# Products over 64 rows of contraction widened to all 128 rows, in a two-layer attention and mLSTM kernel

## The chip, the cores and the metric

The kernel runs on one core of a Trainium2 chip. The metric is the device time of one execution in microseconds (us); smaller is better. The engines of the core are called PE (TensorE, matrix products), DVE (VectorE), ACT (ScalarE), POOL (GpSimd) and SP (SyncE, which issues the DMAs).

## The reference

Two layers over 512 latent tokens and 256 context tokens of width 1024. Layer 0 mixes tokens by two kinds of attention side by side (8 heads of MLA, and 8 query heads of GQA over 2 key heads of dimension 64), layer 1 by a bidirectional mLSTM of 8 heads with keys of dimension 64 and values of dimension 128. Each layer ends with a gated convolutional FFN. Only the latent tokens are returned. The parts that matter here:

```python
def gqa(q, k, v):                        # per key head: 4 query heads, d = 64
    s = einsum('bqgrd,bsgd->bgrqs', q, k) * 64 ** -0.5
    return einsum('bgrqs,bsgd->bqgrd', softmax(s), v)

# mLSTM, one chunk of one direction; C, n is the state before the chunk
s   = einsum('bhtd,bhsd->bhts', qc, kc) * exp(logw - m_t)
num = w_inter * einsum('bhvd,bhtd->bhtv', C, qc) + einsum('bhts,bhsv->bhtv', s, vc)
den = w_inter * einsum('bhd,bhtd->bht', n, qc) + sum(s)
h   = num / max(abs(den), exp(-m_t))
```

## The kernel before

Every operand of a product is held as two tiles, a high part rounded to the matmul's format and a low part with what is left (`split`, L39). A full product of two such operands takes three passes: high by high, low by high and high by low. Projections (`fm`, L78, and `tm`, L89) do this with 128 rows of contraction in each pass.

Where the contraction is only 64 long (a head's dimension in GQA and the mLSTM), two of the three passes are done at once: the query tile holds the high part in 64 rows and the low part in the other 64 (`QE` and `QO` in GQA; the tiles `q` of each head of a pair in the mLSTM), and the high key tile (`KH`, `k`) holds the same high key in both halves. One product with 128 rows gives (high + low) query by high key. The third pass, high query by low key, is a product with 64 rows: `KL` in GQA, `kl` in the mLSTM, and `Sl`, the low part of the mLSTM's state. For even heads the high query stands in rows 0 to 63, for odd heads in rows 64 to 127, and the low tile's half is chosen to match. In GQA `kprep` (L667) already writes the low key to both halves: DVE makes rows 0 to 63 (L675), POOL copies them to 64 to 127 (L676). In the mLSTM one tile `kl` holds the low keys of two heads, one in each half (L925), and `Sl` (L1195) is filled in the half of its head.

The attention (`attend`, L484) is a software pipeline of units; a unit is 256 queries of one head, and a head has two latent units (keys of all 768 tokens) and one context unit (256 keys). Per block of 128 queries a unit makes the scores in PSUM (L424), the negated row maximum on DVE (L427), the exponentials on ACT (L432), a reciprocal on DVE (L434) and the scaling on POOL (L435). Two units later PE transposes the weights (L447), which ACT and DVE split, and three units later PE multiplies them by the values (L469). Between units PE makes the projections that MLA needs next (L95). All 8 GQA heads come first, then the 8 MLA heads, whose scores have 96 rows of contraction and three passes.

The mLSTM (`odd`, L866) works on one head in chunks of 128 tokens: `m_intra` makes the weights within the chunks (a mask from the tiles `tri` is added in PSUM at L1144; the key products are L1154), `m_state` the states before each chunk, and `m_inter` (L1204) the numerators: six products within the chunk (L1212), one by the high state (L1214) and one by the low (L1215). Projections of the next pair of heads and parts of the output projection lie between them as fills (L85, L95, L1103).

A scheduler behind the tile framework sets the order of the instructions on each engine and the semaphores they wait for. Tiles of a pool take over the space of earlier tiles, and where they do, the first writer waits for the last user of that space.

Of the kernel before, what the change touches and what calls it, by code (L numbers as in the profile page):

```python
# [10 lines left out]
F32R = mybir.dt.float32r  # L11
I32 = mybir.dt.int32
BF16 = mybir.dt.bfloat16
# [3 lines left out]
PSUM = bass.MemoryType.PSUM  # L17
SUB, ADD, MUL, MAX, MIN = ALU.subtract, ALU.add, ALU.mult, ALU.max, ALU.min
# [10 lines left out]
def f32(ap):  # L29
    return ap.bitcast(F32)  # L30


class Kernel:
# [14 lines left out]
    def wtile(self, tag, n, cols, dt):  # L48
        """A weight tile: some buffers are permanent, one more of each kind (pool wx) is there when there is room."""
        bufs = [(self.wp, tag + "0"), (self.wp, tag + "1"), (self.wx, tag + "x")]  # L50
        if tag == "wr":
            del bufs[1]
        if self.wx is None:
            bufs.pop()
        self.turn[tag] = self.turn.get(tag, -1) + 1
        pool, nm = bufs[self.turn[tag] % len(bufs)]
        return pool.tile([128, n, cols], dt, tag=nm, name=tag, bufs=1)
# [54 lines left out]
    def B(self, tags):  # L112
        """A PSUM bank, in turn one of the tags: tiles of one tag are taken in program order."""
        self.turn[tags] = self.turn.get(tags, -1) + 1
        tag = tags[self.turn[tags] % len(tags)]
        return self.pp.tile([128, 512], F32, tag=tag, bufs=1, name="ps" + tag)

# [34 lines left out]
    def first_norm(self, pool, X, hh, hl):  # L152
# [63 lines left out]
        # the query projection for GQA goes along, chunk by chunk: one bank for each token tile  # L216
# [78 lines left out]
    def ffn(self, l, X, hh, hl, pool, nt, extra, swap=None, after=None):  # L295
# [4 lines left out]
        a = {}  # L300
        ytile = lambda: pool.tile([128, D], F32, tag="y", name="y", bufs=3)[:, 0:nt]

        def up(f):
            # before the first down products all banks are free for these
            alone = f < 4 and f % 2 == 1

            def banks(tags):
                if alone:
                    return [self.B(tg)[:, 0:n] for tg, (_, n) in zip(tags, segs)]
                p = self.A()  # L310
                return [p[:, t0:t0 + n] for t0, n in segs]

            def halves(ps):
                if nt == T or f >= 4:
                    return [(p, t0, n) for p, (t0, n) in zip(ps, segs)]
                return [(ps[0][:, t0:t0 + n], t0, n) for t0, n in seg2]

            g, v = banks("TU"), banks("RO")
            self.fm(halves(g), self.weights(i["wup"][l, f, 0], KD, 128), (hh, hl), KD)
            self.fm(halves(v), self.weights(i["wup"][l, f, 1], KD, 128), (hh, hl), KD)  # L320
            y = ytile()
            self.conv(y, g, [cw[:, j, f:f + 1] for j in range(3)], cb[:, f:f + 1], segs)
            nc.scalar.activation(y, y, AF.Silu)
            for p, (t0, n) in zip(v, segs):
                nc.vector.tensor_tensor(y[:, t0:t0 + n], y[:, t0:t0 + n], p, op=MUL)
            ah = pool.tile([128, nt], F32R, tag="ah", name="ah", bufs=8)
            al = pool.tile([128, nt], F32R, tag="al", name="al", bufs=8)
            self.split(ah, al, y)
            a[f] = (ah, al)
# [37 lines left out]
        for gi, fs in enumerate(groups):  # L367
            while done < min(NF, fs[-1] + 2):
                up(done)
                done += 1  # L370
                if extra:
                    # its scratch is a y tile, so that it keeps pace with the ups
                    extra.pop(0)(pool.tile([128, D], F32, tag="y", name="y", bufs=3))
            if gi == len(groups) - 1 and swap:
                swap()
            down(fs, gi == len(groups) - 1)
# [122 lines left out]
    def even_tables(self):  # L499
# [4 lines left out]
        # rope tables with the gains folded in  # L504
# [35 lines left out]
    def even(self, hh, hl, acc):  # L540
# [12 lines left out]
        # GQA, token-major  # L553
# [47 lines left out]
        # latents, feature-major  # L601
# [45 lines left out]
        # rope for the shared key part  # L647
# [12 lines left out]
        # while there is little room, the scores' exponentials take the place of the third weight buffers  # L660
# [19 lines left out]
        # GQA attention  # L680
        units = []
        for pr in range(4):
# [20 lines left out]
            units += self.head_units(lambda hd=hd, kv=kv: [(hd["q"][0], KH[kv]), (hd["q"][0][0:64], KL[kv][0:64])],  # L703
                                     V, OT, 4 + pr, 0, {3: [lambda prep=prep: prep([(0, NL)])],
                                                        2: [lambda prep=prep: prep([(NL, NX)])]})
            units += self.head_units(lambda hd=hd, kv=kv: [(hd["q"][1], KH[kv]), (hd["q"][1][64:128], KL[kv][64:128])],
                                     V, OT, 4 + pr, 64)

        # MLA inputs, in steps of one token tile
# [41 lines left out]
        def kvpair(p, pd):  # L751
            k = VM = ss = wk = None

            def step(t):
                nonlocal k, VM, ss, wk
                if t == 0:
                    wk = self.weights(i["w_kvb"][p], 2, 256, kvag)
                    # the keys also go to the space of the query latents, of which both groups are made by then,
                    # the values there and to that of the GQA values
# [56 lines left out]
        # MLA attention: the space of the first head is that of the GQA queries, of the others that of the GQA heads  # L816
# [49 lines left out]
    def odd(self, hh, hl, OT, RP, HP, xs):  # L866
        nc, i = self.nc, self.i
        H = (hh, hl)
        # gates: rows i_f 0.., f_f 32.., i_b 64.., f_b 96..
# [9 lines left out]
        # exponents are kept where the source comes no later (backward: no earlier) than the target; sources on partitions  # L879
        self.tri = []  # L880
        for sg in (1, -1):
            m = RP.tile([128, NT, 128], BF16, tag=f"tri{sg}", name="tri")
            nc.vector.memset(m, 0.0)
            nc.gpsimd.affine_select(m, m, pattern=[[0, NT], [sg, 128]], base=0, channel_multiplier=-sg,
                                    compare_op=ALU.is_ge, fill=-1.0e30)
            self.tri.append(m.rearrange("p q t -> p (q t)"))
# [9 lines left out]
        nc.sync.dma_start(cbs, i["ml_cb"])  # L896
        def proj(hp, pd):
            def qk(w01):
# [4 lines left out]
                if w01:  # L903
                    pd["kl"] = QP.tile([128, NL], F32R, tag="kl", name="kl", bufs=1)
                pd["qk"[w01]] = tiles
                for t0, m in segs:
# [4 lines left out]
                    # twice silu(y), as y (1 + tanh(y / 2))  # L911
# [3 lines left out]
                    for j, (a, b) in enumerate(((slice(0, 64), slice(64, 128)), (slice(64, 128), slice(0, 64)))):  # L915
# [3 lines left out]
                        if w01 == 0:  # L919
                            nc.scalar.mul(t[a], y[a], 0.5)  # L920
                            nc.vector.scalar_tensor_tensor(t[b], y[a], 0.5, f32(t[a]), op0=MUL, op1=SUB)
                        else:
                            nc.scalar.mul(t[a], y[a], 0.0625)
                            nc.gpsimd.tensor_scalar(t[b], y[a], 0.0625, 1.0, op0=MUL, op1=MUL)
                            nc.vector.scalar_tensor_tensor(pd["kl"][a, t0:t0 + m], y[a], 0.0625, f32(t[a]), op0=MUL, op1=SUB)  # L925
                if w01:
                    # the keys with tokens on partitions
# [6 lines left out]
            def v(t):  # L934
                if t == 0:
                    pd["wv"] = self.weights(i["w_mv"][hp], KD, 256)
                    # with a column of ones, which gives the sums
# [21 lines left out]
        with self.tc.tile_pool(name="gates", bufs=1, reuse_waits="tile") as GP:  # L959
# [54 lines left out]
            # per row and tile: the exponents of the weights in the state (ctx as one chunk) and of its decay  # L1014
# [15 lines left out]
            # in the order of the tokens: rows of the backward direction turn round  # L1030
# [34 lines left out]
        # slots of a quarter of a head: the fills make the projections, the gates and the first part of the output  # L1065
# [7 lines left out]
        # from here on nothing reads the normed input: its space takes X and the gated heads  # L1073
# [59 lines left out]
    # the mLSTM of one head, in chunks of 128 tokens, with ctx as one chunk that only makes the first state  # L1133
    def m_intra(self, h, pool, heads, pds, oh, MX, Y, WI, EM, SW, DEC):
        """Within the chunks: the weighted scores, sources on partitions, for both directions."""
# [14 lines left out]
        passes = ((pd["k"][j], pd["q"][j]), (pd["kl"][a], pd["q"][j][a]))  # L1150
# [11 lines left out]
    def m_state(self, h, pool, heads, pds, oh, MX, Y, WI, EM, SW, DEC):  # L1162
        """The states before each chunk of both directions, with the sums in the last column."""
# [28 lines left out]
        Sh, Sl = [pool.tile([128, 4, 2, 130], F32R, tag=f"S{x}", name="S" + x, bufs=1) for x in "hl"]  # L1192
# [5 lines left out]
    def m_inter(self, h, q, pool, heads, pds, oh, MX, Y, WI, EM, SW, DEC):  # L1198
        """One chunk: the part within it plus the state's, for both directions."""
# [15 lines left out]
        nc.tensor.matmul(o, pd["q"][j][a, c], Sl[a, q].rearrange("p d v -> p (d v)"), start=False, stop=True)  # L1215
# [4 lines left out]
    def m_norm(self, h, pool, heads, pds, oh, MX, Y, WI, EM, SW, DEC):  # L1220
        """The numerators over the denominators, both directions summed."""
# [14 lines left out]
    def m_scale(self, h, pool, heads, *_):  # L1236
        """The norm of each token of a head."""
# [19 lines left out]
    def build(self):  # L1257
        tc, nc, i = self.tc, self.nc, self.i
        with ExitStack() as es:
# [54 lines left out]
            # layer 0 mixer  # L1314
# [20 lines left out]
            # layer 0 FFN  # L1335
# [40 lines left out]
            # layer 1 mixer  # L1376
# [26 lines left out]
            # layer 1 FFN  # L1403
# [108 lines left out]
```

## Time and profile before

| | us |
|---|---|
| median of 3 runs | 1812.19 |
| lowest, highest run | 1805.2, 1812.53 |
| span of the profiled execution | 1806.8 |

The page gives no time of the profiled execution beside its span.

| engine | busy us | share of the span | instructions |
|---|---|---|---|
| PE | 1735.2 | 96% | 9615 |
| DVE | 1247.4 | 69% | 2285 |
| ACT | 737.5 | 41% | 1369 |
| POOL | 325.6 | 18% | 357 |

The mean granted clock of PE is 0.977 of full speed. In order of time: conditioning and the first norm to about 165, GQA to about 322, MLA to about 450, the output projection and the FFN of layer 0 to about 1090, gates and first projections of layer 1 to 1158, the mLSTM to 1400, then the last output products and the FFN of layer 1. In the chain of work that ended last, PE has 74% of the span, DVE 10%, POOL 6% and ACT 5%.

A matmul row shows the start, the duration and, as "64*128 64x512", the rows and columns of the weights and of the streamed operand. Durations of matmuls overlap, since they are pipelined, so two neighbouring starts tell more than a duration. In a table by stretch, busy time is given for each engine, with the number of instructions.

### The profile page before, as it was taken

The numbers are of one execution on the slowest core, as the hardware profiler recorded it, in microseconds if no ns is written. First come the engines' busy times: TensorE is split into PE (matmuls) and PEld (weight loads), VectorE is DVE, ScalarE is ACT, GpSimd is POOL, SyncE is SP. The second block draws the span as 40 slices with busy tenths as digits, with TensorE's granted clock in tenths as the row PEclk, the third lists the DMA queues.
The fourth block names the chain that finished last, engine by engine and source line by source line (L and its number), as shares of the span: only waits on it lengthen the run. The fifth ranks groups of instructions, "written<-read, shape, count | busy, mean of one in ns | idle before, by whom it ended". The sixth has DMA issues, their size and how long they took to land.

```text
span 1806.8 us, 25310 instructions
## 1 busy us (share of the span) xinstructions
PE 1735.2 (96%) x9615; PEld 1461.1 (81%) x9622; DVE 1247.4 (69%) x2285; ACT 737.5 (41%) x1369; POOL 325.6 (18%) x357
## 2 busy tenths in 40 slices
PE   6898989999999999999999998999999999999998
PEld 1687768888878888888888887788887898888886
DVE  6896687998868658575867548777777854544444
ACT  3333677889333222121212225645444442232231
POOL 5733254544140000000000005112010210000000
PEclk9898899999999999999999999899998999999999
DMA  8341000000625335242534222111112222323232
GB/s 282 132 153 44 10 11 3 23 1 28 252 71 175 118 105 162 90 151 87 164 106 129 70 73 80 47 48 47 59 35 84 82 94 94 95 94 103 94 103 84
DMA packets 68317, 166.28 MB, mean 92 GB/s; under 512 B 8290, under 2 KB 30818, under 8 KB 67810
## 3 DMA queue, kind: packets, MB, share of 16 engines
q1 hardware_dynamic: 68194, 164.66, 28.2%
q8 instruction: 76, 1.25, 0.3%
q14 instruction: 45, 0.37, 0.1%
q10 hardware_dynamic: 2, 0.01, 0.0%
HBM read 160.44 MB, written 4.20 MB: 91 GB/s over the span
## 4 chain that ended last, share of the span: by engine, by line
PE 74%; DVE 10%; POOL 6%; ACT 5%; issue 4%; DMA 1%; SPq 0%; POOLq 0%; ACTq 0%; DVEq 0%
PE psS L85 30%; PE psT L343 7%; PE psU L343 7%; PE psU L85 3%; PE S L424 3%; PE psR L85 3%; PE psT L85 2%; PE psO L469 2%; PE psR L95 2%; PE psR L343 2%; PE psO L343 2%; PE psU L95 1%; PE psT L95 1%; POOL hl L281 1%; PE psU L1103 1%
## 5 line engine op out<-in xcount | busy, mean ns | idle before, releaser
L85 PE MATMUL psS<-hl,wh 128*128 128x512 f32 (+1 forms) x992 | 348.4, 352 | 3.5 <-POOL hl L281 3.3
L85 PE MATMUL psS<-hh,wh 128*128 128x512 f32 (+1 forms) x992 | 347.1, 351 | 0.4 <-ACT hh L277 0.4
L85 PE MATMUL psS<-hh,wl 128*128 128x512 f32 (+1 forms) x992 | 347.0, 350 | 0.0
L42 ACT CAST wh<-wr 128x1024 fp32r<-128x1024 f32 (+2 forms) x187 | 193.5, 1036 | 358.6 <-PE psO L343 141.3
L43 DVE TENSOR_TENSOR wl<-wr,wh 128x1024 fp32r<-128x1024 f32 (+2 forms) x187 | 229.5, 1228 | 49.4 <-ACT wh L42 48.8
L85 PEld LDWEIGHTS psS<-hl,wh 128*128 128x128 f32 x992 | 187.3, 189 | 31.5 <-POOL hl L281 5.8
L85 PEld LDWEIGHTS psS<-hh,wh 128*128 128x128 f32 x992 | 187.4, 189 | 26.3 <-ACT hh L277 0.7
L85 PEld LDWEIGHTS psS<-hh,wl 128*128 128x128 f32 x992 | 187.4, 189 | 25.3
L291 DVE SCALAR_TENSOR_TENSOR y<-psS,fcw,y 128x511 f32<-128x511 f32 (+1 forms) x60 | 39.5, 658 | 145.5 <-ACT y L289 145.5
L138 DVE CUSTOM_DVE_ANT_0 y<-ar,cb 128x1024 f32<-128x1024 f32 x112 | 136.5, 1219 | 0.0
L261 POOL TENSOR_TENSOR sa<-sa,sq 128x256 f32<-128x256 f32 (+1 forms) x18 | 18.3, 1017 | 648.2 <-ACT sq L260 648.2
L289 ACT ACTIVATE y<-psS,fcb,fcw 128x512 f32<-128x512 f32 (+1 forms) x60 | 40.3, 705 | 207.2 <-PE psS L85 207.2
L378 DVE SCALAR_TENSOR_TENSOR X<-psU,mod,X 128x512 f32<-128x512 f32 (+1 forms) x69 | 48.0, 696 | 91.8 <-PE psU L343 78.9
L435 POOL TENSOR_SCALAR p<-p,rs 128x768 f32<-128x768 f32 (+1 forms) x96 | 73.9, 775 | 134.1 <-DVE rs L434 92.2
L138 DVE CUSTOM_DVE_ANT_0 junk<-ar,cb 128x1024 f32<-128x1024 f32 x64 | 84.0, 1313 | 0.4
L343 PE MATMUL psT<-ah,wh 128*128 128x512 f32 (+1 forms) x184 | 71.7, 390 | 2.2 <-DVE X L378 1.2
L343 PE MATMUL psU<-ah,wh 128*128 128x512 f32 (+1 forms) x184 | 71.5, 388 | 1.2 <-DVE X L378 1.2
L343 PE MATMUL psU<-ah,wl 128*128 128x512 f32 (+1 forms) x184 | 71.0, 386 | 0.0
L343 PE MATMUL psT<-ah,wl 128*128 128x512 f32 (+1 forms) x184 | 71.0, 386 | 0.0
L343 PE MATMUL psT<-al,wh 128*128 128x512 f32 (+1 forms) x184 | 70.9, 386 | 0.0
L343 PE MATMUL psU<-al,wh 128*128 128x512 f32 (+1 forms) x184 | 70.8, 385 | 0.0
L427 DVE TENSOR_REDUCE nm<-S 128x1 f32<-128x768 f32 x64 | 60.3, 946 | 15.0 <-PE S L424 14.7
(664 smaller groups left out, 4387.7 us busy)
## 6 DMA issues: line engine op xcount, KB each, us to landing
ar<-in_ada SPq DMA_DIRECT2D x88, 512.0 KB, 3.6
wr<-in_wup SPq DMA_DIRECT2D x88, 512.0 KB, 3.5
wr<-in_wdn SPq DMA_DIRECT2D x44, 512.0 KB, 3.4
pr<-in_adak SPq DMA_DIRECT2D x16, 256.0 KB, 6.5
wr<-in_w_out SPq DMA_DIRECT2D x8, 512.0 KB, 3.6
wr<-in_w_mqk SPq DMA_DIRECT2D x8, 512.0 KB, 3.4
wr<-in_w_mv SPq DMA_DIRECT2D x8, 512.0 KB, 3.6
wr<-in_w_mo SPq DMA_DIRECT2D x8, 512.0 KB, 3.5
```

What stands on the lines that cost most here:

```text
L42: nc.scalar.copy(hi, src)
L43: nc.vector.tensor_tensor(lo, src, f32(hi), op=SUB)
L85: nc.tensor.matmul(ps, a, b[:, k, x0:x0 + n], start=i == 0, stop=i == 3 * nk - 1)
L95: nc.tensor.matmul(ps, a[:, k, t * 128:(t + 1) * 128], b, start=i == 0, stop=i == 3 * nk - 1)
L138: nc.vector.tensor_tensor_reduce(out, raw, self.cb[:, c], 1.0, 0.0, MUL, ADD, self.mraw[l][:, n, c:c + 1])
L289: nc.scalar.activation(y[:, t0:t0 + n], p, AF.Identity, bias=b, scale=w[1])
L291: nc.vector.scalar_tensor_tensor(y[:, t0 + 1:t0 + n], p[:, 0:n - 1], w[0], y[:, t0 + 1:t0 + n], op0=MUL, op1=ADD)
L343: nc.tensor.matmul(ps[:, 0:n], x[:, off:off + 128], y[:, t0:t0 + n], start=m == 0, stop=m == 3 * nf - 1)
L378: self.nc.vector.scalar_tensor_tensor(X[:, o, t0:t0 + n], ps[:, 0:n], self.mod[l][:, g0 + o, c:c + 1], X[:, o, t0:t0 + n], op0=MUL, op1=ADD)
L424: nc.tensor.matmul(s[:, c0:c0 + n], q[:, q0:q0 + 128], k[:, k0 + c0:k0 + c0 + n], start=m == 0, stop=m == len(passes) - 1)
L427: nc.vector.tensor_reduce(nm, s[:, 0:nk], axis=AX.X, op=MAX, negate=True)
L435: nc.gpsimd.tensor_scalar(p[:, 0:nk], p[:, 0:nk], r, 1.0, op0=MUL, op1=MUL)
```

## The change

The low products of GQA, the low key products and the low state products of the mLSTM are issued over all 128 rows. In GQA both halves of `KL` hold the same low key, so the product also takes in low query by low key. In the mLSTM two tiles `kl` and two tiles `Sl` (one of each for even and one for odd heads) are made once and live through the layer; the half that a head does not write is set to zero once, by POOL. `Sl` no longer comes from the pool of the heads' tiles, and there are two of them in turn where there was one. The mask `tri` is kept for one chunk of 128 columns and not four, and read four times over as a broadcast operand.

The diff also removes comments and docstrings, which are left out here; line numbers after the change are up to 9 higher.

```diff
@@ even
-            units += self.head_units(lambda hd=hd, kv=kv: [(hd["q"][0], KH[kv]), (hd["q"][0][0:64], KL[kv][0:64])],
+            units += self.head_units(lambda hd=hd, kv=kv: [(hd["q"][0], KH[kv]), (hd["q"][0], KL[kv])],
...
-            units += self.head_units(lambda hd=hd, kv=kv: [(hd["q"][1], KH[kv]), (hd["q"][1][64:128], KL[kv][64:128])],
+            units += self.head_units(lambda hd=hd, kv=kv: [(hd["q"][1], KH[kv]), (hd["q"][1], KL[kv])],
@@ odd
-            m = RP.tile([128, NT, 128], BF16, tag=f"tri{sg}", name="tri")
+            m = RP.tile([128, 128], BF16, tag=f"tri{sg}", name="tri")
             nc.vector.memset(m, 0.0)
-            nc.gpsimd.affine_select(m, m, pattern=[[0, NT], [sg, 128]], base=0, channel_multiplier=-sg,
+            nc.gpsimd.affine_select(m, m, pattern=[[sg, 128]], base=0, channel_multiplier=-sg,
                                     compare_op=ALU.is_ge, fill=-1.0e30)
-            self.tri.append(m.rearrange("p q t -> p (q t)"))
+            self.tri.append(m.unsqueeze(1).to_broadcast([128, NT, 128]))
...
+        half = lambda j: slice(64 - 64 * j, 128 - 64 * j)
+        self.kl = [RP.tile([128, NL], F32R, tag=f"kl{j}", name="kl") for j in range(2)]
+        self.Sl = [RP.tile([128, 4, 2, 130], F32R, tag=f"Sl{j}", name="Sl") for j in range(2)]
+        for j in range(2):
+            nc.gpsimd.memset(f32(self.kl[j][half(j)]), 0.0)
+            nc.gpsimd.memset(f32(self.Sl[j][half(j)]), 0.0)
...
-                    pd["kl"] = QP.tile([128, NL], F32R, tag="kl", name="kl", bufs=1)
+                    pd["kl"] = self.kl
...
-                            nc.vector.scalar_tensor_tensor(pd["kl"][a, t0:t0 + m], y[a], 0.0625, f32(t[a]), op0=MUL, op1=SUB)
+                            nc.vector.scalar_tensor_tensor(self.kl[j][a, t0:t0 + m], y[a], 0.0625, f32(t[a]), op0=MUL, op1=SUB)
@@ m_intra
-        passes = ((pd["k"][j], pd["q"][j]), (pd["kl"][a], pd["q"][j][a]))
+        passes = ((pd["k"][j], pd["q"][j]), (pd["kl"][j], pd["q"][j]))
@@ m_state
-        Sh, Sl = [pool.tile([128, 4, 2, 130], F32R, tag=f"S{x}", name="S" + x, bufs=1) for x in "hl"]
+        Sh, Sl = pool.tile([128, 4, 2, 130], F32R, tag="Sh", name="Sh", bufs=1), self.Sl[j]
@@ m_inter
-        nc.tensor.matmul(o, pd["q"][j][a, c], Sl[a, q].rearrange("p d v -> p (d v)"), start=False, stop=True)
+        nc.tensor.matmul(o, pd["q"][j][:, c], Sl[:, q].rearrange("p d v -> p (d v)"), start=False, stop=True)
```

The order of the instructions on PE is the same, row by row. What differs there is a wait, at the first products of GQA (`S` is the score tile, `QE` the queries of an even head):

```order
 L693 MATMUL psU<-ident,QR 128x128
 L424 MATMUL S<-KH,QE 128x512 [waits DVE_49]
-L424 MATMUL S<-KL,QE 128x512
+L424 MATMUL S<-KL,QE 128x512 [waits Pool_49]
 L424 MATMUL S<-KH,QE 128x256
-L424 MATMUL S<-KL,QE 128x256
+L424 MATMUL S<-KL,QE 128x256 [waits Pool_49]
 L424 MATMUL S<-KH,QE 128x512
 L424 MATMUL S<-KL,QE 128x512
```

Nothing moved; the first two low products now wait for POOL as well.

On POOL, at the norm in front of layer 1 (`sa` is the sum of squares of the norm; `Id`, `Fd`, `rm` and `rn` are tables of the gates that are cleared), the piece of the difference reads:

```order
 L261 TENSOR_TENSOR sa<-sa,sq 128x256 [waits Activation_49]
-L965 MEMSET Id 64x768 [waits PE_49]
-L965 MEMSET Fd 64x768
-L965 MEMSET rm 64x768
+L974 MEMSET Id 64x768 [waits DVE_49,PE_49]
+L974 MEMSET Fd 64x768
+L974 MEMSET rm 64x768
 L261 TENSOR_TENSOR sa<-sa,sq 128x256 [waits Activation_49,Pool_49]
```

The order is the same; the clearing of `Id` lies in other space and waits for DVE and for another product of PE.

Later on POOL, between the end of that norm (`hl`) and the first keys (`qk`) of the mLSTM, before:

```order
L281 TENSOR_TENSOR hl<-v,hh 128x256 [waits Activation_49,Pool_49]
L884 AFFINE_SELECT tri<-tri 128x512 [waits DVE_49] x2
L924 TENSOR_SCALAR qk<-cy 64x512 [waits DVE_49,Pool_49]
L924 TENSOR_SCALAR qk<-cy 64x512
L1168 TENSOR_TENSOR kw<-kt,SW 128x768 [waits DVE_49,Activation_49,Pool_49]
```

and after:

```order
L281 TENSOR_TENSOR hl<-v,hh 128x256 [waits Activation_49,Pool_49]
L903 MEMSET kl 64x512 [waits DMAHW6_49,DMAHW1_49,Pool_49]
L884 AFFINE_SELECT tri<-tri 128x128 [waits DVE_49,Pool_49]
L884 AFFINE_SELECT tri<-tri 128x128 [waits DVE_49]
L904 MEMSET Sl 64x1040 [waits Pool_49]
L903 MEMSET kl 64x512
L904 MEMSET Sl 64x1040 [waits PE_49]
L933 TENSOR_SCALAR qk<-cy 64x512 [waits DVE_49]
```

Four clearings are new in front of the keys, and the masks are a quarter as wide.

## Rows read from the trace of the kernel before

**Rows 1.** Timeline of PE in MLA: start us, us, engine, line, operation, tiles, shapes.

```profile
339.43 0.28 PE L424 MATMUL S<-th,tl 96*128 96x256 f32 x1
339.55 0.28 PE L424 MATMUL S<-tl,th 96*128 96x256 f32 x1
```

**Rows 2.** Timeline of PE in GQA, at full clock.

```profile
210.19 0.38 PE L424 MATMUL psR<-KL,QO 64*128 64x256 f32 x1
210.19 0.38 PE L424 MATMUL S<-KL,QE 64*128 64x256 f32 x1
210.50 0.50 PE L424 MATMUL S<-KH,QE 128*128 128x512 f32 x1
210.93 0.50 PE L424 MATMUL S<-KL,QE 64*128 64x512 f32 x1
211.36 0.38 PE L424 MATMUL S<-KH,QE 128*128 128x256 f32 x1
211.67 0.38 PE L424 MATMUL S<-KL,QE 64*128 64x256 f32 x1
```

**Rows 3.** Stretches: us; PE, PEld, DVE, ACT, POOL busy (instructions); clock, DMA, GB/s.

```profile
171.60:196.00 24.40, 24.40 (x58) 15.47 (x59) 11.20 (x26) 9.63 (x21) 4.54 (x6) 0.52 0.00 0
196.00:212.00 16.00, 15.97 (x95) 12.39 (x93) 10.15 (x20) 12.09 (x27) 5.10 (x6) 1.00 0.01 2
212.00:247.00 35.00, 29.91 (x182) 23.27 (x181) 32.07 (x72) 26.12 (x65) 17.38 (x22) 1.00 0.04 12
247.00:303.00 56.00, 55.45 (x307) 43.33 (x307) 40.92 (x94) 40.89 (x99) 24.57 (x30) 0.97 0.04 9
303.00:322.00 19.00, 17.17 (x108) 13.38 (x109) 18.41 (x45) 13.93 (x36) 11.00 (x13) 1.00 0.05 16
1158.00:1400.00 242.00, 238.46 (x1397) 201.67 (x1405) 177.25 (x366) 117.70 (x262) 38.44 (x37) 0.97 0.17 53
```

**Rows 4.** Timeline of PE in GQA, at the lower clock.

```profile
184.64 0.79 PE L424 MATMUL S<-KL,QE 64*128 64x512 f32 x1
185.36 0.58 PE L424 MATMUL S<-KH,QE 128*128 128x256 f32 x1
```

**Rows 5.** Stretches, KL alone: us; PE, PEld, DVE, POOL; clock, DMA, GB/s.

```profile
171.60:196.00 24.40, 9.39 (x14) 4.00 (x14) 0.00 (x0) 0.00 (x0) 0.52 0.00 0
196.00:212.00 16.00, 3.45 (x9) 1.47 (x9) 1.00 (x2) 0.24 (x1) 1.00 0.01 2
212.00:247.00 35.00, 6.45 (x17) 2.75 (x16) 0.09 (x1) 0.70 (x2) 1.00 0.04 12
247.00:303.00 56.00, 13.54 (x32) 5.83 (x32) 0.00 (x0) 0.00 (x0) 0.97 0.04 9
```

**Rows 6.** Timeline of POOL, with the idle time before and its end in brackets.

```profile
168.84 0.95 POOL L676 CAST KL<-KL 64x512 fp32r<-64x512 f32 x2 [17.05 <-DVE KL L675]
...
1134.60 1.70 POOL L924 TENSOR_SCALAR qk<-cy 64x512 fp32r<-64x512 f32 x2 [17.74 <-DVE cy L914]
```

**Rows 7.** Timeline of PE in the mLSTM.

```profile
1355.52 0.33 PE L1154 MATMUL psT<-qk,kl 64*128 64x128 f32 x1
1355.77 0.33 PE L1154 MATMUL psT<-qk 128*128 128x128 f32 x1
...
1363.62 0.33 PE L1214 MATMUL num<-Sh,qk 128*128 128x260 f32 x1
1363.89 0.38 PE L1215 MATMUL num<-Sl,qk 64*128 64x260 f32 x1
1364.20 0.33 PE L1212 MATMUL num<-V,Dh 128*128 128x130 f32 x1
```

**Rows 8.** Timeline of PE and POOL at the norm in front of layer 1.

```profile
1088.37 0.73 POOL L965 MEMSET Id<- 64x768 f32 x1
...
1089.12 0.28 PE L343 MATMUL psU<-ah,wl 128*128 128x256 f32 x1
...
1091.42 0.73 POOL L261 TENSOR_TENSOR sa<-sa,sq 128x256 f32<-128x256 f32 x1 [0.96 <-ACT sq L260]
```

## The prediction

> **What bounds the kernel now.** The page says TensorE (PE) is busy for 96% of the span, and that share hides the question, because a matmul that waits for the array to drain counts as busy. So I read the timeline of PE first and look at starts, not at durations. Where all neighbours use the same rows, the next matmul starts as soon as the array has taken the columns of the last: 0.12 us apart for 256 columns, with 96 rows of contraction [rows 1]; 512 columns then take 0.24. The low-key products of GQA use 64 rows between products that use 128, and there the starts are 0.43 us apart behind a 512-column product and 0.31 behind a 256-column one, both on the way in (KH to KL) and on the way out (KL to KH) [rows 2]. Each change of the number of rows costs 0.19 us in which no column enters.
>
> Next I read the busy times by stretch, since a gain on PE is worth nothing where another engine sets the pace. In the GQA attention (171.6 to 322) PE is busy nearly throughout, but VectorE (DVE) is at 32.07 of 35 us in 212 to 247 and at 18.41 of 19 in 303 to 322, while it has slack in the other stretches [rows 3]. In the mLSTM (1158 to 1400) PE is busy 238.46 of 242 us against 177.25 for DVE and 117.70 for ScalarE (ACT) [rows 3]: the end of that stretch is PE's alone.
>
> **The change part by part.**
>
> *GQA low keys.* The code makes 80 such products (8 heads: 2 halves, 2 blocks, 2 column pieces each, and 2 context blocks). They take all 128 rows afterwards, and the rows were already filled (KL is copied to both halves before and after), so no operation is added; the instruction order of PE is the same. What goes is 80 entries and 80 exits. At full clock a 512-column product gives back 0.43 + 0.43 - 2 x 0.24 = 0.38 us, a 256-column one 0.31 + 0.31 - 2 x 0.12 = 0.38 [rows 1, 2]. In 171.6 to 196 the granted clock is 0.52 [rows 3], so nearly always the lower level of 1.2 GHz; the step out is 0.72 us there [rows 4], and with the step in alike and the pace doubled to 0.48 the price is 0.48. The counts by stretch are in [rows 5]; the last stretch has the 8 left of the 80. Stretch by stretch, against what the next engine allows:
> - 171.6 to 196: 14 x 0.48 = 6.7 us. DVE and ACT are under half busy, so I take all of it. Below: 4, if the start-up latency of the first units shows. Above: what is left, 17.7 us, is at the lower clock; if it all came at the higher, 8.8 more.
> - 196 to 212: 9 x 0.38 = 3.4; ACT has 12.09 us of work there, so 3.0.
> - 212 to 247: 17 x 0.38 = 6.5, but DVE's 32.07 us of work at 0.97, the highest share that these rows show (303 to 322), still needs 33.1: at most 1.9, at least 0; I take 1.0.
> - 247 to 303: 32 x 0.38 = 12.2; DVE and ACT have 40.9 us each, at a share of 0.92 (that of 212 to 247) 44.5, so at most 11.5. Two engines near that share rarely interleave perfectly: 10.
> - 303 to 322: 8 x 0.38 = 3.0, DVE already at 0.97: 0.
>
> Together 20.7 of 31.8 us. The cover that is gone is PE's own slowness: what is late next is DVE (row maxima, splits of the transposed weights) and ACT (exponentials).
>
> *The new wait of the first low product on POOL.* The 128-row product reads the copied half of KL too. POOL makes both pieces of that copy from 168.84 on, 0.95 us [rows 6]; the products start at 171.6. Cost 0, and for the second key head the copy is made well ahead in the same way.
>
> The Trainium skill speaks against this change at one point: its page "TensorE: Matmul & The Clock Gate", section "Part 3: Packing small matmuls — row/col tiling", says that products in different row groups run side by side in the array. The trace agrees where it can happen: at 210.19 a low product on rows 64 to 127 and one on rows 0 to 63 start in the same hundredth of a microsecond [rows 2]. By that rule the pair shared one entry and one exit and the change loses 0.38 + 0.12 = 0.5 us at such a place. It needs two low products in a row, and the order nearly always puts a high one between them, so the sum by the rule is 0.5 to 1 us less.
>
> *mLSTM low keys and low states.* 8 heads of 4 chunks give 32 products each. Low keys: 0.25 us out [rows 7], taken as much in, against 0.12, the pace for up to 256 columns [rows 1]: 0.26 x 32 = 8.3. Low states: 0.27 in and 0.31 out [rows 7], 0.58 - 0.24 = 0.34, x 32 = 10.9. Sum 19.2. All of it is on PE, and PE has no other engine over it on the whole: DVE's 177.25 us would be 0.80 of what is left. In short pieces DVE is ahead, so I take nine tenths, 17.3; below, 12, if a third turns into waits for DVE.
>
> *The zeroed tiles.* POOL gets four memsets. One of 64x768 takes 0.73 us [rows 8], so 64x512 is about 0.5 and 64x1040 about 1.0: 3.0 us in all, less what the smaller masks save. They stand before L924, ahead of which POOL is idle for 17.74 us [rows 6]: cost 0, and 3.0 if that cover were gone. No later clearing is needed, since only one half is ever rewritten.
>
> *The mask as a broadcast operand* (16 matmuls). No row shows a moving operand of this kind that repeats. It has the same 512 columns; nearest is the plain 512-column pace of 0.24 us. Between -1 and +4 us if each took as long again; I take 0.
>
> *The moved addresses.* The clearing of Id on POOL now waits for DVE and for a later product of the first FFN, by the built program's count the second into its last psU, at 1089.12 + 0.28 = 1089.40, instead of starting at 1088.37 [rows 8]. Behind it on POOL stand two more clearings and the sum of squares at 1091.42, which the norm and then the mLSTM's projections wait for. 1089.4 plus three times 0.7 is 1091.5: 0.1 us late; at most 1.0. On SP the gate bias now waits for PE and not POOL, for a product that is done before, and the weight queue behind it has the same waits as before.
>
> **The sum.** 20.7 + 17.3 - 0.1 = 37.9 us off the profiled execution, whose span is 1806.8 us: 1768.9. The page gives no time for that execution other than its span; the median of the three runs is 1812.2, 5.4 above it, and I carry the difference: 1812.2 - 37.9 = 1774.
>
> **The rivals.**
> - *Attention goes over to DVE and ACT altogether.* For it: DVE at 0.92 and 0.97 in two stretches, and units that hand over through four engines. Against it: 24.4 + 16 us with little DVE work and 56 at 0.73. Then about 4 + 2 + 0 + 4 there and 15 in the mLSTM: 25 us, 1787.
> - *Everything counts, and the clock too.* Denser products bring the higher clock back sooner than at 196, and DVE follows: 31.8 + 19.2 and half of the 8.8, 55 us, 1757. Against it: 303 to 322.
> - *Slower: the clock.* PE, now ahead, waits for DVE between short bursts in 196 to 322, and the lower clock of the first 24 us of attention comes back and stays. That stretch has 126 us less 66 x 0.38, about 100 us of PE work. Every part at the lower clock costs as much again, so 40% of it eats the 38 us, and 60% gives 1812 + 22 = 1834. Against it: the stretches 212 to 247 and 303 to 322 have such waits now, at a clock of 1.00 [rows 3].
> - *The change doesn't do what it says*: the wide starts come from the reading of KL or Sl and not from the number of rows, and stay. Then 1812. Against it: the step out of a low product is as long as the step in, and the low keys of the mLSTM, another tile, show it too [rows 7].
>
> **How the numbers follow.** Chances: forecast 0.66 (own range 1764 to 1784), attention bound by DVE 0.17, everything counts 0.12, no effect 0.02, slower 0.03. The range goes to the first two rivals with the bounds of the unknown costs: 1753 (the 55 us and the other half of the 8.8) to 1791 (25 us, less the 4 of the mask). A measurement of this kernel tells about 0.5%, 9 us, from no change. Faster by more: 0.66 + 0.17 + 0.12 = 0.95; within: 0.02; slower: 0.03.
>
> **What would show it.** KL, kl and Sl products appear with 128 rows; starts behind them at 0.24, 0.12 and 0.12 us; 1158 to 1400 shorter by 15 to 19 us with PE still busy throughout; 171.6 to 322 shorter by 17 to 25 with DVE over 0.85 of it and idle time of PE in front of transposes and value products. Wrong would be starts still 0.3 us apart, a granted clock near 0.5 beyond the first 20 us of attention, or any change between 322 and 1080.

## The result, and the profile after

The changed kernel takes 1777.35 us (median of 4 runs, 1774.55 to 1780.44), the kernel before 1809.74 on the same chip: ratio 0.9823, 95% interval 0.9800 to 0.9846, 32.4 us less. A second series gave 1780.57 against 1812.63: 0.982 (0.9804 to 0.9836). The forecast was 1774, in 1753 to 1791.

From the page after, the busy times (share of the span, instructions):

```profile
PE 1685.1 (95%) x9622; PEld 1443.6 (81%) x9622; DVE 1246.0 (70%) x2285; ACT 737.0 (41%) x1369; POOL 327.2 (18%) x361
```

PE lost 50.1 us of busy time while the span lost 30.5. The other engines do what they did; in the chain that ended last PE has 69% for 74 and DVE 13% for 10. The steps answer to [rows 2]. Timeline of PE in GQA after:

```profile
199.23 0.28 PE L424 MATMUL psR<-KL,QO 128*128 128x256 f32 x1
199.35 0.28 PE L424 MATMUL S<-KL,QE 128*128 128x256 f32 x1
199.47 0.40 PE L424 MATMUL S<-KH,QE 128*128 128x512 f32 x1
199.70 0.40 PE L424 MATMUL S<-KL,QE 128*128 128x512 f32 x1
199.94 0.28 PE L424 MATMUL S<-KH,QE 128*128 128x256 f32 x1
```

Starts are 0.23 and 0.24 us apart behind 512 columns and 0.12 behind 256, where they were 0.43 and 0.31. In the mLSTM, answering to [rows 7]:

```profile
1328.55 0.27 PE L1163 MATMUL psT<-qk 128*128 128x128 f32 x1
1328.66 0.28 PE L1163 MATMUL psT<-qk,kl 128*128 128x128 f32 x1
1328.78 0.28 PE L1163 MATMUL psT<-qk 128*128 128x128 f32 x1
...
1335.27 0.33 PE L1223 MATMUL num<-Sh,qk 128*128 128x260 f32 x1
1335.44 0.28 PE L1224 MATMUL num<-Sl,qk 128*128 128x260 f32 x1
1335.57 0.23 PE L1221 MATMUL num<-V,Dh 128*128 128x130 f32 x1
```

Low keys go at 0.11 in and out (0.25 before), low states at 0.17 in and 0.13 out (0.27 and 0.31). The stretches of [rows 3], bounded by the same instructions, the first from the first low product on (us; PE, PEld, DVE, ACT, POOL busy; clock, DMA share, GB/s):

```profile
173.67:186.34 12.67, 11.25 (x58) 10.15 (x57) 9.67 (x25) 8.77 (x21) 4.55 (x6) 0.83 0.00 1
186.34:201.07 14.73, 13.92 (x95) 12.06 (x94) 10.62 (x21) 12.17 (x27) 5.06 (x6) 1.00 0.01 2
201.07:236.34 35.27, 27.24 (x181) 23.95 (x181) 32.30 (x74) 26.30 (x65) 17.41 (x22) 0.95 0.04 12
236.34:283.87 47.53, 44.62 (x308) 40.20 (x306) 40.46 (x92) 39.77 (x97) 24.20 (x30) 1.00 0.04 11
283.87:304.39 20.52, 16.90 (x108) 14.36 (x108) 19.26 (x49) 15.52 (x42) 11.41 (x14) 0.92 0.04 14
...
1139.30:1370.90 231.60, 218.50 (x1405) 193.78 (x1404) 177.10 (x365) 117.30 (x261) 38.30 (x37) 0.97 0.17 55
```

I laid the starts of the same PE instructions of the traces side by side, since the first product of attention, behind code that no run changes, starts anywhere from 170.1 to 177.8 us in the fourteen traces. What each stretch gained, us:

| stretch before | forecast | changed | second series |
|---|---|---|---|
| 171.6 to 196 | 6.7 | 11.1 | 11.9 |
| 196 to 212 | 3.0 | 1.5 | 1.5 |
| 212 to 247 | 1.0 | -0.3 | 0.9 |
| 247 to 303 | 10 | 8.4 | 8.4 |
| 303 to 340 | 0 | -0.9 | -0.9 |
| 340 to 1150 | 0 | 0.0 | 0.0 |
| 1150 to 1400 | 17.3 | 10.9 | 11.1 |

GQA gave 19.8 and 21.8 us of the 20.7 forecast, the mLSTM 10.9 and 11.1 of 17.3. In the mLSTM PE is some 20 us less busy, but idle for 13.1 us and not 3.5. PE's waits there (us in total, times, longest), first before, then after:

```profile
PE kt L930 <- DVE cy L914: 1.7, 5, 0.7
PE state L1181 <- DVE num L1218: 1.0, 1, 1.0
PE psT L1154 <- DVE OT L1254: 0.7, 1, 0.7
```

```profile
PE kt L939 <- DVE cy L923: 3.5, 5, 1.1
PE state L1190 <- DVE V L43: 1.8, 3, 0.6
PE psT L1262 <- DVE hn L1256: 1.7, 3, 1.0
PE psR L95 <- DVE cy L292: 1.6, 2, 0.8
PE state L1190 <- DVE num L1227: 1.5, 1, 1.5
PE psT L1163 <- DVE OT L1263: 1.2, 1, 1.2
PE num L1223 <- ACT Sh L1203: 0.8, 1, 0.8
```

The same three hand-overs last longer, and three new ones of 1.6 us or more stand beside them, all from DVE; the longest one from another engine is the 0.8 us from ACT. Theory A: DVE's queue, not a lack of PE work, took back some 9 us of the mLSTM's gain. Rival: an unlucky execution, or chains of dependent instructions that no queue lengthens.

POOL, answering to [rows 6, 8] (idle time before and its end in brackets):

```profile
170.32 0.95 POOL L676 CAST KL<-KL 64x512 fp32r<-64x512 f32 x2 [15.55 <-DVE KL L675]
...
1116.05 1.84 POOL L933 TENSOR_SCALAR qk<-cy 64x512 fp32r<-64x512 f32 x2 [15.16 <-DVE cy L923]
```

The copy of KL ends 2.4 us before the products at 173.67. `Id` waits 1.04 us for PE at 1070.99, yet the sum of squares stands at 1073.05, 18.4 us earlier than before, exactly what PE is ahead there: nothing lost. The new clearings lie ahead of 15.16 idle us.

### The profile page after: what moved, and what is told of

Its sections match the earlier page's. It is cut to its first block, busy times and chain, and to the rows that moved or that the text cites. A ratio compares the mean times of both kernels' runs of the same rounds, so it can differ in the third digit from the quotient of the medians.

```text
span 1776.3 us, 25328 instructions
## 1 busy us (share of the span) xinstructions
PE 1685.1 (95%) x9622; PEld 1443.6 (81%) x9622; DVE 1246.0 (70%) x2285; ACT 737.0 (41%) x1369; POOL 327.2 (18%) x361
## 4 chain that ended last, share of the span: by engine, by line
PE 69%; DVE 13%; ACT 7%; POOL 6%; issue 3%; DMA 1%; SPq 0%; POOLq 0%; ACTq 0%; DVEq 0%
PE psS L85 30%; PE psT L343 7%; PE psU L343 7%; PE psU L85 4%; PE psR L85 3%; PE psT L85 2%; PE psO L343 2%; PE psR L343 2%; PE S L424 1%; ACT p L432 1%; PE psO L469 1%; POOL hl L281 1%; DVE junk L138 1%; PE psR L95 1%; PE state L1190 1%
## 5 line engine op out<-in xcount | busy, mean ns | idle before, releaser
L325 DVE TENSOR_TENSOR y<-y,psS 128x512 f32<-128x512 f32 (+1 forms) x60 | 34.1, 597 | 52.5 <-PE psS L85 52.4
```

## The experiments

**GQA alone, the mLSTM alone, the tiles alone.** The kernel before, with only the first, only the second, or only the third of these:

```
- (hd["q"][0], KH[kv]), (hd["q"][0][0:64], KL[kv][0:64])
+ (hd["q"][0], KH[kv]), (hd["q"][0], KL[kv])                # GQA alone
- (pd["kl"][a], pd["q"][j][a])      Sl[a, q]
+ (pd["kl"][j], pd["q"][j])         Sl[:, q]                # mLSTM alone, with the tiles below
+ self.kl, self.Sl once per parity, halves zeroed; tri [128, 128] broadcast   # tiles alone, 64 rows kept
```

> The kernel before with the GQA part of the change alone. My theory (a change of the number of rows costs PE about 0.19 us, nothing else matters): the stretch 171.6 to 322 of the kernel before gets 19 to 21 us shorter, as in the changed kernel, and nothing else moves: 19 to 21 us faster. Rival (the gain of that stretch came from a clock that happened to come back sooner in the profiled execution): about 10 us faster. Rival (the parts help each other): clearly less than 19.

> The kernel before with the mLSTM part alone (low keys, low states, two tiles each, narrow mask). My theory: 20 us of PE's busy time go in 1158 to 1400 and 9 to 10 come back as idle time in front of work that DVE releases: 10 to 12 us faster. Rival (the loss against the 19.2 us worked out before comes from the clock in one profiled execution, not from DVE): 15 to 19 us faster.

> The mLSTM part without its point: two tiles kl and Sl, cleared halves, narrow mask and moved addresses, but the products still read 64 rows; GQA as before. My theory: no change, within 2 us. Rival (a second Sl tile lets DVE write the next state sooner, and that is where the mLSTM's gain comes from): 5 to 10 us faster. Rival (the clearings and moved waits cost): 1 to 5 us slower.

Before was 1811.88. GQA alone: 1789.23, ratio 0.9875 (0.9856 to 0.9894), 22.6 us less; its trace gains 22.0 between 171.6 and 340, and 1.35 in 1150 to 1400, where it changes nothing. The tiles alone: 1808.87, 0.9987 (0.9967 to 1.0006): no change. The mLSTM alone: 1795.1, 0.9907 (0.9889 to 0.9925), 16.8 us less, more than I expected and in the rival's range. Its trace:

```profile
1155.41:1386.18 230.77, 217.15 (x1404) 192.90 (x1403) 177.04 (x365) 117.39 (x261) 38.33 (x37) 0.98 0.18 56
```

Here too PE is idle for 13.6 us, and the mLSTM gains 11.7 us. The other 5 lie elsewhere: 1.9 in the first 24 us of attention, which this kernel doesn't change (the clock, below), and 3 because the profiled execution of before is that far under the median of these runs. So the rival fits the time but not the trace; the two single parts together (39.4) exceed the whole by a difference of this kind.

**The second series of the changed kernel.**

> The changed kernel once more, as the base for the three runs beside it. Expected 1776 to 1782 us, ratio 0.980 to 0.984 against the kernel before. Theory A (the low states and low keys of the mLSTM lose 17 to 20 us of PE work and PE gets 9 to 10 us of that back as idle time in front of hand-overs from DVE) expects the same idle times in the mLSTM as in its first trace, some 13 us. Rival (the mLSTM's gain of 10.9 us instead of 17.3 was one unlucky execution) expects another 5 us or more to be gone in this trace between the first intra product of head 1 and 1371.

```profile
1141.65:1373.06 231.41, 218.48 (x1405) 194.44 (x1404) 177.03 (x365) 117.29 (x261) 38.31 (x37) 0.97 0.18 55
```

Idle time 12.9 us, gain 11.1: the loss repeats, and the unlucky execution is out.

**Fewer changes, still 64 rows.** In the kernel before, the passes go outside the loop over columns or chunks, so that low products stand side by side:

```
-            for c0 in range(0, nk, 512):
-                n = min(512, nk - c0)
-                for m, (q, k) in enumerate(passes):
+            for m, (q, k) in enumerate(passes):
+                for c0 in range(0, nk, 512):
+                    n = min(512, nk - c0)
```

> The kernel before with its 64-row products unchanged in number and rows, but issued next to each other: in GQA both high products of a block and then both low ones, in the mLSTM four high key products and then four low ones. The latent units of GQA go from 64 single low products to 32 pairs, the low keys of the mLSTM from 32 singles to 8 groups of four. My theory (the price is per change of rows): 32 x 0.38 = 12 us and 24 x 0.26 = 6 us of PE time go; with the shares that came through in the changed kernel (two thirds and a half) 10 to 12 us faster. Rival (a 64-row product is slow in itself, or its operands are): no change, within 2 us.

1802.6, ratio 0.9948 (0.9929 to 0.9966), 9.4 us less. By the trace it isn't the plain proof I wanted: 4.2 us come in 1150 to 1400, 1.3 in 196 to 303, and 8.4 in the first 24 us of attention, where the clock is in play. (They add up to 13.9, less 1.0 lost behind attention, while the spans of the two traces differ by 7.1 only: the attention of this one execution began 5.7 us later.) Rows of that stretch for before, this run and the changed kernel (last numbers: clock, DMA share, GB/s):

```profile
171.40:195.20 23.80, 23.60 (x54) 14.68 (x55) 10.84 (x26) 9.02 (x20) 4.54 (x6) 0.50 0.00 0
```

```profile
177.10:183.80 6.70, 6.48 (x17) 4.74 (x18) 4.09 (x11) 3.41 (x6) 0.90 (x1) 0.50 0.00 0
```

```profile
171.20:178.00 6.80, 4.92 (x15) 4.54 (x16) 5.58 (x17) 4.97 (x9) 0.67 (x2) 0.50 0.00 0
178.00:195.30 17.30, 15.83 (x109) 14.32 (x109) 13.69 (x28) 12.69 (x30) 5.73 (x8) 1.00 0.01 2
```

With single low products PE stays at the lower level (1.2 GHz) for 23.8 us, though it never pauses; with grouped or wide ones it is back at 2.4 GHz after 7 (a granted clock of 1.00 from 183.9 and from 178.0). The three traces with single low products in GQA have 20 to 24 us at the lower level here, the eleven others 3.4 to 6.8. The trace with 20 (the mLSTM alone) has them in two pieces of 10.2 us with 3.4 us at 2.4 GHz between, so single low products don't always keep the clock down; why it rose there stays open.

**The price by itself, where nothing waits.** In the FFN of layer 1, where PE is busy 200 of 200 us, one or two of the three passes over 192 blocks take 64 rows:

```
-                    nc.tensor.matmul(ps, a, b[:, k, x0:x0 + n], ...)
+                    r = slice(0, 64) if half and i % 3 in (1,) else slice(0, 128)     # or (1, 2)
+                    nc.tensor.matmul(ps, a[r], b[r, k, x0:x0 + n], ...)
```

> The changed kernel, with one 64-row product put between 128-row products at 192 places of the FFN of layer 1 (up products of 12 of its blocks, second pass over rows 0 to 63 only, so half of that low pass is left out). In this stretch PE is busy 200.0 of 200 us. Theory (each change of the number of rows costs PE 0.19 us at full clock, whatever the kernel, and where PE waits for nothing it all counts): 192 x 2 x 0.19 = 73 us more than the changed kernel, some 1850 to 1856 us. Rival (only part of such steps counts, as in the mLSTM, where 10.9 of 19 us came out): some 40 us more, 1815 to 1825 us.

> As the run before it, with two adjacent 64-row products at each of the 192 places (second and third pass, so half of both low passes is left out): twice the products, as many changes of the number of rows. Price per change: again 73 us more than the changed kernel, 1850 to 1856 us, and equal to the run before within 4 us. Price per 64-row product: 146 us more, some 1925 us.

One 64-row product: 1856.42, 0.4 over the range expected; two: 1854.75; the kernel before beside them 1809.44, so the changed one by its ratio 1776.9. Timelines of PE, one, then two; in the second the loads of the weights are shown too (PEld):

```profile
1499.38 0.39 PE L86 MATMUL psS<-hh,wh 128*128 128x512 f32 x1
1499.70 0.50 PE L86 MATMUL psS<-hh,wl 64*128 64x512 f32 x1
1500.13 0.50 PE L86 MATMUL psS<-hl,wh 128*128 128x512 f32 x1
1500.46 0.39 PE L86 MATMUL psS<-hh,wh 128*128 128x512 f32 x1
```

```profile
1500.70 0.18 PEld L86 LDWEIGHTS psS<-hh,wl 64*128 64x128 f32 x1 [0.35 <-issue]
1500.70 0.49 PE L86 MATMUL psS<-hh,wl 64*128 64x512 f32 x1
1500.81 0.19 PEld L86 LDWEIGHTS psS<-hl,wh 64*128 64x128 f32 x1
1501.04 0.39 PE L86 MATMUL psS<-hl,wh 64*128 64x512 f32 x1
1501.36 0.19 PEld L86 LDWEIGHTS psS<-hh,wh 128*128 128x128 f32 x1 [0.36 <-issue]
1501.36 0.50 PE L86 MATMUL psS<-hh,wh 128*128 128x512 f32 x1
1501.79 0.50 PE L86 MATMUL psS<-hh,wl 64*128 64x512 f32 x1
```

Three products take 1.08 or 1.09 us and not 0.68 (three of 0.227): 0.40 for one narrow product and 0.41 for two. Times 192 that is 77 and 78 us; the starts behind the stretch are 76.8 and 78.2 later. The price is one per pair of changes, whether one narrow product stands between them or two, and here all of it is paid in time.

The PEld rows show where it goes. Behind a product with as many rows, the load of the weights starts 0.23 us ahead of its product (1500.81 and 1501.04) and lies under the product before. At a change between 128 and 64 rows the load and its product start together (1500.70, 1501.36), and so it is at all of the 192 changes each way in both runs, and at 243 changes at full clock in the trace of before, within 4 ns. A load takes 0.18 to 0.19 us, which is what a change costs in GQA. That this bare load is the whole of the price is a reading of the rows; no run takes it apart.

A change between 128 and 96 rows costs nothing. In the trace of before, in MLA:

```profile
348.14 0.28 PE L95 MATMUL psU<-wh,CK 128*128 128x256 f32 x1
348.15 0.19 PEld L424 LDWEIGHTS S<-th 96*128 96x128 f32 x1
348.26 0.40 PE L424 MATMUL S<-th 96*128 96x512 f32 x1
```

The 96-row product starts 0.12 us behind a 256-column one of 128 rows, the pace without a change [rows 1], with its load 0.11 us ahead. By the medians of such steps behind 256 columns at full clock, the way in takes 0.120 us (31 steps) and the way out 0.121 (32).

**DVE relieved in the mLSTM.** Without 18 of the low weight splits:

```
-                self.split(hi, lo, raw)
+                nc.scalar.copy(hi, raw)      # lo = hi; queries, keys, values of heads 2 to 7 and gates
```

> The changed kernel without the low parts of 18 weight blocks of the mLSTM (queries, keys, values of heads 2 to 7 and their gates; PE multiplies by the high part in their place, as many products as before, so the low part is left out of the result). It takes some 15 DVE instructions of 1.22 us, 18 us of DVE's 177, out of the mLSTM's stretch, and nothing from PE. Theory A (PE gets its gain back there as idle time because DVE's queue is late): PE's idle time in the mLSTM falls from 13 to 4 to 8 us and the kernel takes 5 to 9 us less than the changed kernel, ratio to the kernel before 0.977 to 0.980. Rival (each of these waits is the length of a chain of dependent instructions over ACT and DVE to PE, whatever stands in DVE's queue): idle time within 2 us of 13 and the time within 2 us of the changed kernel, 0.981 to 0.983.

1770.94, ratio 0.9789 (0.9769 to 0.9809), 6 us less than the changed kernel's 0.982.

```profile
1139.55:1363.53 223.98, 216.28 (x1409) 193.52 (x1408) 159.50 (x350) 116.41 (x262) 35.30 (x37) 0.98 0.18 57
```

With 17.6 us less in DVE's queue PE idles for 7.7 us and not 13.1, and the stretch is 7.6 shorter (the other 2.2 come from the clock, 0.98). The waits for `V` and the conv's `cy` (L292) are gone: those were queue. The five for `kt` (3.3 us for 3.5), and those for `num` (1.5) and `OT` (1.2), hardly move: those the rival has right. Time and idle time are where theory A expected them; the interval just touches the changed kernel's (0.9804 to 0.9836), and the trace agrees with it.

**Single hand-overs relieved.** Post-splits of three heads on POOL; the transposes of the keys behind the first value products; half of each low state on POOL (this one with the next experiment's edit):

```
+ nc.gpsimd.tensor_scalar(OT[:, h], OT[:, h], og2[:, h:h + 1], 1.0, op0=MUL, op1=MUL)   # h = 1, 3, 5
+ nc.gpsimd.tensor_tensor(x[1], OT[:, h], f32(x[0]), op=SUB)
```

```
+                if t == 0:
+                    kt()          # six transposes and their copy, out of qk(1) into v(0)
```

```
+ nc.gpsimd.tensor_tensor(Sl[a, 2:4], S[:, 2:4], f32(Sh[0:64, 2:4]), op=SUB)
```

> The changed kernel, with the split of the attention output of heads 1, 3 and 5 (at about 1337 to 1342 us, six DVE instructions of 0.74 us, line 46) made on ACT and POOL instead of ACT and DVE. Theory A (DVE's queue holds PE back here: the normalised head 0.98 us, the product sum 1.48 us, and then 10.24 us at the lower clock) expects both waits to shrink and 2 to 5 us less than the changed kernel. Rival (PE then waits as long at the next hand-over) expects a difference within 1.5 us.

> The changed kernel, with the transposes of the mLSTM keys (kt, line 939) issued behind the first value products of their pair of heads instead of in front of them. In the changed kernel PE waits for DVE's last key instruction five times, 3.5 us in all, with value products queued behind that need nothing from DVE. Theory A (each such wait is worth its length) expects these waits to go and 2.5 to 3.5 us less than the changed kernel. Rival (DVE's throughput sets the pace, and the time comes back at the next hand-over) expects a difference within 1 us; a later state product that waits for the keys would make it slower by 1 to 3 us.

> The rotation of MLA's queries on POOL, as in the run that took 5.6 us off the changed kernel (1774.97 us), and besides the second half of each low state of the mLSTM subtracted on POOL (eight times 0.75 us of DVE). Theory A (DVE's queue holds PE back in the mLSTM): 1 to 3 us less, 1771 to 1774 us. Rival (no queue, or POOL's half comes later than DVE's did): 1775 to 1783 us.

The splits on POOL: 1780.46 against 1780.57, nothing; the wait for `hn` shrank, and that for `num` grew from 1.5 to 2.8 us.

The keys later: 1794.19, 13.6 us slower than the second series, against both theories and far past the 1 to 3 us allowed for a late state product. The waits for `kt` went; in their place came

```profile
PE num L1227 <- DVE num L1233: 9.7, 3, 4.0
```

with a stretch at a mean clock of 0.92. By the code, the transposes and the chunk products take turns in the same two PSUM buffers, which DVE's `num` has to read out first; that the new turn of the buffers is the cause is my reading, and no run tests it. The low states on POOL: 1784.14, 0.986 (0.984 to 0.988), worse than the next experiment by 0.7%, and worse than the changed kernel (0.982); here `hn` is what is late (4.0 us of waits for 1.7).

None of the three shortened the stretch. But the two moves to POOL didn't relieve DVE, so they say little about its queue. The stretch of the mLSTM with the splits on POOL, then with the low states there (the changed kernel has DVE at 177.10 and 177.03 us):

```profile
1140.13:1373.03 232.90, 218.54 (x1405) 193.97 (x1403) 177.57 (x362) 117.27 (x261) 45.75 (x43) 0.97 0.17 55
```

```profile
1134.41:1372.99 238.58, 222.62 (x1404) 198.54 (x1403) 180.19 (x365) 117.01 (x261) 49.42 (x45) 0.95 0.17 54
```

In the first, three instructions of 0.74 us left DVE, but its busy time did not fall, since others took longer. In the second, the subtractions took 2.6 us less of DVE, and three of its operations on the sums (`num`, `nn`) 5.0 us more: two `num` operations per head went from 0.69 to 0.89 us each. Why they take longer these runs don't tell.

**DVE relieved in GQA.** The rotation of MLA's queries, 10.3 us of DVE between 219 and 307, on POOL:

```
-                nc.vector.tensor_tensor(qr, qr, Cmq[...], op=MUL)
+                nc.gpsimd.tensor_tensor(qr, qr, Cmq[...], op=MUL)        # and the other two of rope()
```

> The changed kernel, with the rotation of MLA's queries (18 DVE instructions, 10.3 us of DVE between 219 and 307 us) on POOL. DVE is busy 32.3 of 35.3 us from 201 to 236 and 19.3 of 20.5 us from 284 to 304, where GQA gained nothing. Theory (DVE sets the pace of these two stretches, so the change could give nothing there) expects 2 to 6 us less than the changed kernel. Rival (ACT's and POOL's hand-overs end last anyway, and POOL's own scaling of the scores is put off by the new work) expects 0 to 3 us more.

1774.97 against 1780.57, ratio 0.9792 (0.9774 to 0.9810): the fastest version that computes everything, though its interval touches the changed kernel's. Two stretches between the same instructions, the changed kernel's second series first:

```profile
204.59:241.15 36.56, 28.47 (x199) 24.78 (x199) 34.29 (x80) 28.68 (x74) 19.45 (x25) 1.00 0.04 12
...
286.42:308.92 22.50, 18.91 (x123) 16.25 (x122) 21.45 (x54) 16.77 (x45) 12.45 (x16) 0.92 0.05 13
```

```profile
197.22:230.06 32.84, 28.43 (x199) 24.50 (x199) 30.24 (x72) 28.23 (x74) 23.67 (x33) 1.00 0.07 19
...
275.37:294.32 18.95, 17.27 (x122) 14.86 (x122) 16.95 (x46) 15.87 (x43) 12.66 (x20) 1.00 0.06 16
```

In the first, PE's work is the same (28.4 us), DVE has 4.05 less and the stretch is 3.7 shorter: DVE sets its pace. The second is 3.6 shorter, but some 1.7 of that is the clock (1.00 for 0.92), and 1.9 is given back in the 15 us behind it: there the run leaves it open.

## Why the prediction held, and where it didn't

- *The price of a change of rows* was right for the changes that were made: 0.38 us for a pair by [rows 1, 2], 0.40 by itself in the FFN, and the starts are where the forecast put them. "Each change of the number of rows costs 0.19 us" was too wide: between 128 and 96 rows it costs nothing, as the trace of before could have told. What the prediction called draining shows in the rows as a load of weights that does not start ahead of its product. One step was misjudged: a low state of 260 columns takes 0.17 us on the way in, not 0.12. By the medians of all steps at full clock the low keys give (0.257 + 0.254 - 0.113 - 0.111) x 32 = 9.2 us and the low states (0.263 + 0.313 - 0.173 - 0.123) x 32 = 9.0, 18.2 and not 19.2 (0.29 and 0.28 us for a pair).
- *Side by side.* The rule that the prediction weighed from the Trainium skill ("TensorE: Matmul & The Clock Gate", "Part 3: Packing small matmuls — row/col tiling") bears out as small as said: at 199.23 and 199.35 two low products now follow one another by 0.12 us where two started together at 210.19 [rows 2]. From the high product before the two to the one behind them it is 0.47 us now and was 0.63, so this place gave 0.16 and not twice 0.38. The trace of before has one more such place, at 226.40.
- *GQA* gave the forecast sum by another split, and that the sum came out is luck. The first stretch gave 11 to 12 and not 6.7, for the clock came back at 178 and not at 195; the prediction had that only as its upper bound. 196 to 212 and 247 to 303 gave 1.5 and 8.4 of 3.0 and 10, and 303 to 340 lost 0.9, which took the surplus back. That DVE sets the pace in 212 to 247, read from [rows 3], was right, as the rotation on POOL shows; for 303 to 322 that run shows it less clearly.
- *The mLSTM* is the term that was mis-sized: 17.3 forecast, 10.9 and 11.1 measured, 11.7 with the mLSTM alone. PE's work shrank as worked out; "I take nine tenths" failed, and so did the sign I named for it, PE "still busy throughout". The lower bound of 12 ("if a third turns into waits for DVE") was the better reading: half did. DVE's share of the stretch (0.80) was no measure, for PE meets DVE at single hand-overs: seven ended in a wait before, 3.4 us in all, and fifteen in DVE's rows shown do after, 11.3 us. How close behind PE the others came I hadn't looked up. The run without low splits shows DVE's queue to be over half of the added idle time; what would shorten the rest (`kt`, `num`, `OT`) stays open: the later keys made the stretch longer, and the two moves to POOL took no time off DVE.
- *The mask, the zeroed tiles, the copy on POOL, the moved clearing* cost nothing, as said; the tiles alone show the first two.
- *The rivals.* "Attention goes over to DVE" held for 212 to 247, less surely for 303 to 322, and not for the rest. "Everything counts, and the clock too" was right on the clock at the start of attention and wrong on the rest. "Slower by the clock" came in short spells alone: the granted clock was 0.95 and 0.92 in the two stretches where [rows 3] had 1.00 and PE idled, and neither lost more than 1.7 us. "It doesn't do what it says" is refuted by the starts.
- *The sum.* 37.9 forecast, 32.4 measured; the base of 1812.2 was 2.5 above the median beside the runs, so the forecast came out 3.4 low. That is luck in part: the base made up 2.5 of the 5.5 us that were missing, and the mLSTM's term alone was 6 too high.

## What to carry to other kernels

A matmul row that is busy can be waiting: compare starts of neighbours, and see whether the load of the weights starts ahead of its product. Here it didn't at products of 64 rows among products of 128; making them as wide cost nothing, since the other rows were there anyway or could be zeroed once. Before counting such a gain in full, go through the hand-overs of the stretch one by one: in the FFN all of it counted, in the mLSTM a good half. Taking work from the late engine helped where its busy time really fell (the rotation, the low weight splits left out); check that it did, for two moves to POOL left DVE as busy as before, and a change in the order made a longer wait.

## What the runs showed of the hardware

- Two changes between 128 and 64 rows cost 0.40 us around one 64-row product or two of 512 columns, and 0.28 to 0.29 around one of 128 or 260 columns in the mLSTM; changes between 128 and 96 rows cost nothing. In the FFN it is spread over the starts of several products: 0.32, 0.43 and 0.33 us around one, 0.34, 0.32 and 0.43 with two, all 0.227 without. At each change the load of the weights starts with its product, where it otherwise starts up to 0.23 us ahead.
- At the start of attention PE, busy 23.6 of 23.8 us, stayed at the lower clock (1.2 GHz) in the two traces with single 64-row products throughout, and in a third with 3.4 us at 2.4 GHz in the middle; in the eleven with those products grouped or widened it was at 2.4 GHz after 3.4 to 6.8 us. So 4 to 5 of the 11 to 12 us gained there go beyond what the rows of before gave for the changes themselves (6.7).
- DVE's split at 1338.33 took 1.09 us with POOL at work on its own splits, where the same instruction takes 0.74 in the changed kernel with POOL idle; that run does not tell why.
